# A hybrid decoder step on one core: weight sums moved from GpSimd to VectorE, up sums kept unsplit, split down halves kept in scratch, five longer raw buffers

## The chip, the cores and the metric

The kernel runs on one core of one Trainium2 chip. The metric is the device time of one execution in microseconds (us), here the median of three runs. One more execution was recorded by the hardware profiler; all rows below are from it.

## The reference, cut to what matters

The program is one layer of a decoder for 2048 prompt tokens and 8 x 4 sample tokens, width 1024: a mixer (gated linear attention beside a spatial gating unit), cross-attention over 256 memory tokens, and a gated MLP with a causal depthwise convolution over time. The change touches the last of these:

```
def conv_ffn(hn, buf, w_gate, w_up, conv_w, conv_b, w_down):
    T = hn.shape[1]
    g = hn @ w_gate                                   # (T,1024) @ (1024,2816)
    gp = jnp.concatenate([buf.astype(g.dtype), g], axis=1)
    c = conv_b + sum(conv_w[j] * gp[:, j:j + T] for j in range(CONV_W))
    out = (jax.nn.gelu(c) * (hn @ w_up)) @ w_down     # w_up (1024,2816), w_down (2816,1024)
    return out, gp[:, -(CONV_W - 1):]
```

## The kernel before, in words

All data is fp32. A product is made of three TensorE matmuls on split operands (`mm3`, lines 92 to 95): each factor is split into a part rounded to the format that TensorE reads and the rest (`split`, lines 84 to 86: ScalarE makes the high half, VectorE subtracts it to get the low half), and high x high, high x low and low x high are added in PSUM.

The 2048 tokens go through the layer in four blocks of 512 (`s` = 0 to 3); 32 sample tokens ride with block 1 in the mixer and with block 2 in the MLP. A block passes mixer, cross-attention and MLP in turn. The MLP walks over 22 feature tiles of 128 in pairs (`j`) and in groups of four tiles (`GROUPS`): for each pair a gate step and an up step; the down products of a group come between the first gate and the first up step of the next one (`main`, `pend`).

Block 0 computes gate and up plainly (`fm_step`, eight k-tiles times a 512-token moving operand, 128x512 matmuls) from weights that it loads raw (512 KB units, `wload`, line 104) and splits (`wsplit`). Beside that it prepares the weights for blocks 1 to 3 (`wmake`, `seven_make`): these use a seven-product scheme (2x2 blocks of weights and tokens, seven products in place of eight), with three plain weight quadrants A11, A12, A22 and four sums S1 to S4. `seven_make` forms the sums of one raw unit in four operations (lines 152 to 155, on GpSimd, tiles `s13`, `s24`), splits them (`sh`, `sl`), and writes the split quadrants and the split sums into scratch in device memory (`w7d`, lines 160, 161, 166). `seven_step` in blocks 1 to 3 loads each of the seven as a ready tile of split halves (`seven_tile`, line 141), accumulates the products into four quadrants in a tile `Q` (own pool `qp`, two buffers) and hands these on. The down weights are loaded raw and split anew in every block, 22 units each (`down`, `down_last`).

A raw unit needs one of `NRAW` = 3 raw buffers (tag `wraw`); a buffer is free when its last reader is done. Split halves go into five buffers each (`whi`, `wlo`). `run` makes the units of later steps up to five units ahead. All DMAs are issued by SyncE (SP in the rows), in one order. A scheduler sets the order of the instructions on each engine when the program is built; each engine then runs its own list in order. The gate results leave PSUM on VectorE at line 1364 (`gate_put`), the up results at line 1416, the down results at line 1466; a group of PSUM accumulators has four banks (`accp`).

Of the kernel before, what the change touches and what calls it, by code (L numbers as in the profile page):

```python
# [30 lines left out]
NU, NT, NRAW, NW = 49, 6, 3, 5  # L31
# [6 lines left out]
def hymba_step_kernel(  # L38
# [16 lines left out]
    qp = ctx.enter_context(tc.tile_pool(name="qp", bufs=2))  # L55
# [41 lines left out]
    def wraw(name):  # L97
        return wp.tile([128, 1024], F32, tag="wraw", name=f"r_{name}", bufs=NRAW)

    def wload(w, k0, nk, m0, mw, name):  # L100
        raw = wraw(name)
        r3 = raw.rearrange("p (k m) -> p k m", k=nk) if nk * mw == 1024 else \
            raw[:, :nk * mw].rearrange("p (k m) -> p k m", k=nk)
        nc.sync.dma_start(r3, w[k0 * 128:(k0 + nk) * 128, m0:m0 + mw].rearrange("(k p) m -> p k m", p=128))
        return r3
# [27 lines left out]
    W7 = ("A11", "A12", "A22", "S1", "S3", "S2", "S4")  # L133
# [12 lines left out]
    def seven_make(raw, hi, lo, dst, u, name):  # L146
# [5 lines left out]
        pool.tensor_tensor(h3(s13, 0), a21, a22, ALU.add)  # L152
        pool.tensor_tensor(h3(s13, 1), a11, a21, ALU.subtract)
        pool.tensor_tensor(h3(s24, 0), h3(s13, 0), a11, ALU.subtract)
        pool.tensor_tensor(h3(s24, 1), a12, h3(s24, 0), ALU.subtract)
        ks = slice(2 * u, 2 * u + 2)
        for x, t in enumerate((hi, lo)):
            t = t.bitcast(F32).rearrange("p (k two) m -> p two k m", two=2)
            for k in range(2):
                nc.sync.dma_start(dst[:, k, x, ks], t[:, k, :, 0:128])  # L160
            nc.sync.dma_start(dst[:, 2, x, ks], t[:, 1, :, 128:256])
# [25 lines left out]
    def seven_step(src, get_xs, H, use, name, order=0):  # L187
# [3 lines left out]

        def fn(*ws):
            xs, w = get_xs(), dict(zip(seq, ws))
            q = qp.tile([128, 4 * TM // 2], F32, tag="Q", name=f"q_{name}")
# [3 lines left out]
            def prod(nm):  # L198
# [7 lines left out]
                for k in range(len(xs)):  # L206
                    mm3(o, w[nm][:, 0, k], w[nm][:, 1, k], *xs[k][nm], k == 0, k == len(xs) - 1)
# [34 lines left out]
        return Step(fn, [seven_tile(src[:, W7.index(nm)], f"{name}{nm}") for nm in seq])  # L242
# [180 lines left out]
    def run(steps):  # L423
# [5 lines left out]
        for i, st in enumerate(steps):  # L429
# [12 lines left out]
    w7d = {(nm, j): dp.tile([128, 7, 2, 4, 128], F32, tag=f"w7{nm}{j}", name=f"w7{nm}{j}")  # L442
           for nm in ("g", "u") for j in range(FT // 2)}
# [898 lines left out]
    def ffn_steps(B, fin=None):  # L1342
# [36 lines left out]
        def gate7(j):  # L1379
# [8 lines left out]
            return seven_step(w7d["g", j], lambda: B.hn, H, use, f"wg{s}{j}", int(j == 0))  # L1388
# [31 lines left out]
        def upp7(j):  # L1420
# [9 lines left out]
            return seven_step(w7d["u", j], lambda: B.hn, H, use, f"wup{s}{j}")  # L1430

        def down_last(f0, half_of):
# [17 lines left out]
            return Step(fn, [(w_down[0], f0, 2, j * 512, 512, f"wd{s}{f0}{j}") for j in range(2)])  # L1450

        def down(f0, nf, m):
# [17 lines left out]
            return Step(fn, [(w_down[0], f0, nf, m * 128, nm * 128, f"wd{s}{f0}{m}")])  # L1470
# [138 lines left out]
```

## Time and profile before

| | |
|---|---|
| median of 3 runs | 2974.5 us (2973.43 to 2977.55) |
| profiled execution, device time | 2971.9 us |
| its span (first to last instruction) | 2970.2 us |
| TensorE busy | 2880.4 us, 97% of the span |
| VectorE, ScalarE, GpSimd busy | 1815.1, 1073.9, 861.9 us |
| moved by DMA | 614 MB, 207 GB/s over the span |

How to read it: PE is TensorE, PEld its weight loads, DVE VectorE, ACT ScalarE, POOL GpSimd, SP SyncE. An engine's busy time is the union of its instructions; the end of a matmul is modelled, so PE that is busy without a break can still run below its best rate. PEclk is the clock that TensorE was granted, as a share of its full speed. A row that ends in "<-" names what ended the idle time before an instruction. The MLP of block 0 lies between 420 and 820 us of the span, the others between about 1210 and 1600, 1935 and 2290, 2615 and 2970 us.

### The profile page before, as it was taken

The page shows a single profiled execution, that of the slowest core. Times are in us where ns is not written, and L with a number is a line of the kernel's source. Part 1 is how long each engine was busy: PE and PEld are TensorE (multiplying, and loading weights), DVE is VectorE, ACT ScalarE, POOL GpSimd, SP SyncE. Part 2 cuts the span into 40 slices and gives each one's busy share as a digit, 9 for nine tenths or more (in the row PEclk, how much of TensorE's full clock was granted, in tenths as well). Part 3 has the DMA queues.
Part 4 walks back from the last instruction along what each step waited for, and adds up shares of the span by engine and source line. Part 5 has one row for each costly group of instructions (what it writes and reads, how often), then busy time and mean ns, then how long its engine had stood idle before and what let it go on. Part 6 is the DMA issues. An engine that isn't in the chain of part 4 may idle for free.

```text
span 2970.2 us, 47609 instructions
## 1 busy us (share of the span) xinstructions
PE 2880.4 (97%) x18148; PEld 2534.4 (85%) x18148; DVE 1815.1 (61%) x2973; ACT 1073.9 (36%) x1948; POOL 861.9 (29%) x900
## 2 busy tenths in 40 slices
PE   8998999999999999999999999999999999999998
PEld 8787887777778789888887888899999788999997
DVE  6577558776656553654556685575557676375556
ACT  5535335343354332422223543332223543241222
POOL 1123227555422220421221232232222233041221
PEclk9999999999999899999999999999999999999999
DMA  9555679999941135887886323577775323577883
GB/s 286 180 156 159 212 233 286 276 300 295 287 130 57 52 107 176 287 295 258 305 314 200 100 72 125 195 250 252 267 264 182 112 71 108 185 276 256 286 289 127
DMA packets 389580, 613.97 MB, mean 207 GB/s; under 512 B 27195, under 2 KB 269822, under 8 KB 389352
## 3 DMA queue, kind: packets, MB, share of 16 engines
q1 hardware_dynamic: 389352, 610.92, 62.0%
q8 instruction: 144, 2.36, 0.3%
q14 instruction: 84, 0.69, 0.1%
HBM read 497.04 MB, written 113.78 MB: 206 GB/s over the span
## 4 chain that ended last, share of the span: by engine, by line
PE 75%; DVE 9%; DMA 6%; POOL 3%; ACT 3%; issue 3%; SPq 1%; DVEq 0%; POOLq 0%; ACTq 0%
PE d L94 5%; PE d L95 5%; PE d L93 5%; PE sc L94 2%; PE sc L95 2%; PE sc L93 2%; PE a_wo L94 2%; PE a_wo L95 2%; PE a_wo L93 2%; PE s L921 1%; PE a_wx L94 1%; PE a_wx L93 1%; PE a_wx L95 1%; PE a_wu L94 1%; PE a_wu L93 1%
## 5 line engine op out<-in xcount | busy, mean ns | idle before, releaser
L93 PE MATMUL d<-acth,h_wd 128*128 128x512 f32 (+2 forms) x896 | 316.1, 356 | 20.2 <-DVE g L1364 8.8
L94 PE MATMUL d<-actl,h_wd 128*128 128x512 f32 (+2 forms) x896 | 316.1, 353 | 4.7 <-DVE actl L86 4.7
L95 PE MATMUL d<-acth,l_wd 128*128 128x512 f32 (+2 forms) x896 | 315.1, 353 | 0.0
L1466 DVE TENSOR_TENSOR h<-d,h 128x512 f32<-128x512 f32 (+1 forms) x232 | 133.2, 583 | 187.4 <-PE d L95 186.6
L93 PEld LDWEIGHTS d<-acth,h_wd 128*128 128x128 f32 x896 | 170.1, 191 | 48.3 <-DVE g L1364 10.7
L94 PEld LDWEIGHTS d<-actl,h_wd 128*128 128x128 f32 x896 | 171.2, 191 | 28.3 <-DVE actl L86 6.0
L95 PEld LDWEIGHTS d<-acth,l_wd 128*128 128x128 f32 x896 | 171.1, 191 | 24.8 <-issue 2.5
L1427 POOL TENSOR_TENSOR c<-q_wup,c 128x512 f32<-128x512 f32 (+1 forms) x33 | 58.3, 1766 | 424.7 <-DVE q_wup L238 245.6
L1405 POOL TENSOR_TENSOR c<-c,bc_f 128x512 f32<-128x512 f32 (+1 forms) x88 | 129.1, 1469 | 96.3 <-ACT c L1404 87.7
L86 DVE TENSOR_TENSOR l_wd<-r_wd,h_wd 128x1024 fp32r<-128x1024 f32 x88 | 123.1, 1399 | 41.0 <-ACT h_wd L85 29.6
L95 PE MATMUL sc<-whi_qk,wol 128*128 128x256 f32 x512 | 144.1, 282 | 0.0
L93 PE MATMUL sc<-whi_qk,woh 128*128 128x256 f32 x512 | 144.0, 283 | 0.0
L94 PE MATMUL sc<-wlo_qk,woh 128*128 128x256 f32 x512 | 143.7, 282 | 0.0
L85 ACT ACTIVATE h_wd<-r_wd 128x1024 fp32r<-128x1024 f32 x88 | 92.8, 1056 | 124.4 <-PE d L94 45.1
L914 POOL TENSOR_TENSOR e<-e,k 128x512 f32<-128x512 f32 (+1 forms) x48 | 72.6, 1513 | 216.8 <-DVE kr L910 129.4
L1395 ACT ACTIVATE c<-g,colsb 128x512 f32<-128x512 f32 x88 | 71.5, 814 | 156.5 <-DVE g L1364 94.7
L93 PE MATMUL a_wo<-ch,h_wo 128*128 128x512 f32 (+1 forms) x320 | 113.4, 361 | 8.5 <-ACT ch L85 5.9
L94 PE MATMUL a_wo<-cl,h_wo 128*128 128x512 f32 (+1 forms) x320 | 114.4, 358 | 0.1
L95 PE MATMUL a_wo<-ch,l_wo 128*128 128x512 f32 (+1 forms) x320 | 113.7, 356 | 0.0
L1396 DVE SCALAR_TENSOR_TENSOR c<-g,colsb,c 128x512 f32<-128x512 f32 x88 | 90.8, 1032 | 28.7 <-ACT c L1395 27.6
L1392 POOL COPY carry<-g 128x2 f32<-128x2 f32 x88 | 34.7, 394 | 241.4 <-DVE g L1364 237.9
L93 PE MATMUL a_wx<-pTh,whi_wx 128*128 128x512 f32 x256 | 101.3, 396 | 0.0
(3282 smaller groups left out, 9455.8 us busy)
## 6 DMA issues: line engine op xcount, KB each, us to landing
r_wd<-in_w_down_dram SPq DMA_DIRECT2D x88, 512.0 KB
r_wo<-in_w_out_dram SPq DMA_DIRECT2D x32, 512.0 KB
whi_qk<-qkd SPq DMA_DIRECT2D x32, 512.0 KB
wlo_qk<-qkd SPq DMA_DIRECT2D x32, 512.0 KB
wlo_wx<-vod SPq DMA_DIRECT2D x32, 512.0 KB
whi_wx<-vod SPq DMA_DIRECT2D x32, 512.0 KB
r_wg<-in_w_gate_dram SPq DMA_DIRECT2D x22, 512.0 KB
r_wup<-in_w_up_dram SPq DMA_DIRECT2D x22, 512.0 KB
```

The lines of the kernel that those rows point to most:

```text
L85: act.activation(hi, src, AF.Copy)
L86: (lo_eng or dve).tensor_tensor(lo, src, hi.bitcast(F32), ALU.subtract)
L93: pe.matmul(ps, wh, xh, start=first, stop=False)
L94: pe.matmul(ps, wh, xl, start=False, stop=False)
L95: pe.matmul(ps, wl, xh, start=False, stop=last)
L914: pool.tensor_tensor(kl[:, :Tl], e[:, :Tl], B.k[p][:, :Tl], ALU.mult)
L1392: pool.tensor_copy(carry[:, f, :], g[:, SB:SB + 2])
L1395: act.activation(c[:, :SB], g[:, 2:SB + 2], AF.Identity, bias=cb, scale=w2)
L1396: dve.scalar_tensor_tensor(c[:, :SB], g[:, 1:SB + 1], w1, c[:, :SB], ALU.mult, ALU.add)
L1405: pool.tensor_tensor(c[:, :T], c[:, :T], B.fbc[:, :T], ALU.mult)
L1427: (dve, pool)[i].tensor_tensor(c[:, :T], q[i], c[:, :T], ALU.mult)
L1466: dve.tensor_tensor(B.h[m + mm][:, cs], ps[:, :cw], B.h[m + mm][:, cs], ALU.add)
```

## The change

The four sum operations run on VectorE. The sums of the up weights are written to scratch as they are (half the bytes of their split form) and split in each of blocks 1 to 3 when they are loaded again (`seven_sums`: one raw unit of 512 KB holds two sums); those of the gate weights stay split. The down weights are split in block 0 alone; their halves are written to scratch (`wkeep`, 2 x 512 KB per unit) and loaded ready in blocks 1 to 3 (`wready`). The quadrant tile `Q` comes out of the raw pool, which has five buffers of 1088 elements in place of three of 1024 and two `Q` buffers. The core of the diff:

```diff
-NU, NT, NRAW, NW = 49, 6, 3, 5
+NU, NT, NRAW, NW = 49, 6, 5, 5
...
-    qp = ctx.enter_context(tc.tile_pool(name="qp", bufs=2))
...
-        return wp.tile([128, 1024], F32, tag="wraw", name=f"r_{name}", bufs=NRAW)
+        return wp.tile([128, 2 * TM], F32, tag="wraw", name=f"r_{name}", bufs=NRAW)
...
+    def wkeep(dst, *spec):
+        def load():
+            out = wunit(*spec)
+            for x, t in enumerate(out):
+                nc.sync.dma_start(dst[:, x], t.bitcast(F32))
+            return out
+        return load
...
-        pool.tensor_tensor(h3(s13, 0), a21, a22, ALU.add)
-        pool.tensor_tensor(h3(s13, 1), a11, a21, ALU.subtract)
-        pool.tensor_tensor(h3(s24, 0), h3(s13, 0), a11, ALU.subtract)
-        pool.tensor_tensor(h3(s24, 1), a12, h3(s24, 0), ALU.subtract)
+        dve.tensor_tensor(h3(s13, 0), a21, a22, ALU.add)
+        dve.tensor_tensor(h3(s13, 1), a11, a21, ALU.subtract)
+        dve.tensor_tensor(h3(s24, 0), h3(s13, 0), a11, ALU.subtract)
+        dve.tensor_tensor(h3(s24, 1), a12, h3(s24, 0), ALU.subtract)
...
         for i, t in enumerate((s13, s24)):
+            d = sums[:, 2 * i:2 * i + 2]
+            put = lambda d, t: nc.sync.dma_start(d[:, :, ks], t.rearrange("p (s k m) -> p s k m", s=2, k=2))
+            if len(sums.shape) == 4:
+                put(d, t[:, :512])
+                continue
             sh, sl = U(f"sh{i}{name}", F32R), U(f"sl{i}{name}", F32R)
             split(sh[:, :512], sl[:, :512], t[:, :512])
             for x, o in enumerate((sh, sl)):
-                nc.sync.dma_start(dst[:, 3 + 2 * i:5 + 2 * i, x, ks],
-                                  o[:, :512].bitcast(F32).rearrange("p (s k m) -> p s k m", s=2, k=2))
+                put(d[:, :, x], o[:, :512].bitcast(F32))
...
+    def seven_sums(src, name):
+        def load():
+            raw = wraw(name)
+            nc.sync.dma_start(raw[:, :1024], src.rearrange("p s k m -> p (s k m)"))
+            return wsplit(raw[:, :1024].rearrange("p (k m) -> p k m", k=8), name)
+        return load
...
-            q = qp.tile([128, 4 * TM // 2], F32, tag="Q", name=f"q_{name}")
+            q = wraw(f"q_{name}")
...
-            return Step(fn, [(w_down[0], f0, nf, m * 128, nm * 128, f"wd{s}{f0}{m}")])
+            name = f"wd{s}{f0}{m}"
+            return Step(fn, [wready(wdd[f0, m], name) if s else
+                             wkeep(wdd[f0, m], w_down[0], f0, nf, m * 128, nm * 128, name)])
```

The change moves instructions on four engines; three places show how. In block 0, at the start of the down products of one group, GpSimd had the sums of two up units between its other work (`r_wup` raw unit, `c` and `g` tiles of the convolution, `carry` its two last tokens):

```order
L1405 TENSOR_TENSOR c_6239<-c_6239,bc_f_4615 128x512
L152 TENSOR_TENSOR s13wup_6329<-r_wup_6323 128x256
L153 TENSOR_TENSOR s13wup_6329<-r_wup_6323 128x256
L154 TENSOR_TENSOR s24wup_6330<-s13wup_6329,r_wup_6323 128x256
L1392 COPY carry<-g_6378 128x2
L1353 COPY g_6413<-carry 128x2
L155 TENSOR_TENSOR s24wup_6330<-r_wup_6323,s24wup_6330 128x256
L152 TENSOR_TENSOR s13wup_6429<-r_wup_6423 128x256
```

At the same place VectorE's list now holds them, between the gate evictions (line 1364 before, 1408 now), the convolution (1440, 1441) and the low halves of the down weights (`l_wd`):

```order
L1408 TENSOR_TENSOR g_6313<-a_wg_6288,bc_f_4636 128x512
L160 TENSOR_TENSOR s13wup_6274<-r_wup_6268 128x256
L161 TENSOR_TENSOR s13wup_6274<-r_wup_6268 128x256
L162 TENSOR_TENSOR s24wup_6275<-s13wup_6274,r_wup_6268 128x256
L1440 SCALAR_TENSOR_TENSOR c_6317<-g_6313,colsb,c_6317 128x512
L163 TENSOR_TENSOR s24wup_6275<-r_wup_6268,s24wup_6275 128x256
L1441 SCALAR_TENSOR_TENSOR c_6317<-g_6313,colsb,c_6317 128x512
L160 TENSOR_TENSOR s13wup_6364<-r_wup_6358 128x256
L161 TENSOR_TENSOR s13wup_6364<-r_wup_6358 128x256
L85 TENSOR_TENSOR l_wd_6263<-r_wd_6260,h_wd_6262 128x1024
L162 TENSOR_TENSOR s24wup_6365<-s13wup_6364,r_wup_6358 128x256
L1408 TENSOR_TENSOR g_6348<-a_wg_6323,bc_f_4636 128x512
```

Between the two gate evictions there now stand seven sum operations, two convolution steps and one split; a raw unit that lands late holds up what follows on VectorE, and no longer on GpSimd. SyncE's list at the same group, before (raw loads at line 104, writes of the ready tiles `w7g`):

```order
L160 DMA w7g_190<-h_wg_6141 128x2x128 x2
L161 DMA w7g_190<-h_wg_6141 128x2x128
L160 DMA w7g_190<-l_wg_6142 128x2x128 x2
L161 DMA w7g_190<-l_wg_6142 128x2x128
L104 DMA r_wd_6251<-in_w_down_dram 128x4x256
L104 DMA r_wd_6317<-in_w_down_dram 128x4x256
L104 DMA r_wup_6323<-in_w_up_dram 128x4x256
L104 DMA r_wup_6423<-in_w_up_dram 128x4x256
L166 DMA w7u_201<-sh0wup_6341 128x2x256
```

And now (raw loads at line 102, `wd_0`, `wd_2`, ... the kept down halves, line 134):

```order
L134 DMA wd_0_233<-h_wd_6108 128x1024
L102 DMA r_wup_6268<-in_w_up_dram 128x4x256
L134 DMA wd_0_233<-l_wd_6109 128x1024
L102 DMA r_wup_6358<-in_w_up_dram 128x4x256
L134 DMA wd_2_234<-h_wd_6186 128x1024
L134 DMA wd_2_234<-l_wd_6187 128x1024
L102 DMA r_wg_6406<-in_w_gate_dram 128x4x256
L134 DMA wd_4_235<-h_wd_6194 128x1024
L134 DMA wd_4_235<-l_wd_6195 128x1024
L102 DMA r_wg_6464<-in_w_gate_dram 128x4x256
L172 DMA s7u_208<-s13wup_6274 128x2x256
```

Both up units and both following gate units are now issued ahead of the writes of the first up unit's sums; before, the two gate units came behind these. In blocks 1 to 3 the four raw down loads of a group (for one group of block 2 they stood in a row) become eight loads into split buffers, with the raw sums of the next up steps (line 203) among them:

```order
L203 DMA r_wup24S_19853<-s7u_200 128x1024
L148 DMA wg24S_19721<-s7g_198 128x1024
L148 DMA wg24A_19719<-w7g_197 128x1024
L148 DMA wg24A_19723<-w7g_197 128x1024
L124 DMA whi_wd_19725<-wd_0_229 128x1024
L124 DMA wlo_wd_19727<-wd_0_229 128x1024
L124 DMA whi_wd_19729<-wd_2_230 128x1024
L124 DMA wlo_wd_19731<-wd_2_230 128x1024
L203 DMA r_wup24S_19993<-s7u_200 128x1024
L203 DMA r_wup25S_20243<-s7u_204 128x1024
```

The first raw sums of an up step stand ahead of the down halves of the group before, the second ones behind two of the four units. TensorE's instructions are the same in number and nearly the same in order.

## Rows read from the trace of the kernel before

**Rows 1.** The page's busy time of each engine, whole span.

```profile
PE 2880.4 (97%) x18148; PEld 2534.4 (85%) x18148; DVE 1815.1 (61%) x2973; ACT 1073.9 (36%) x1948; POOL 861.9 (29%) x900
```

**Rows 2.** Windows: stretch, length, busy us of each engine, PEclk, DMA share, GB/s.

```profile
420.00:820.00 400.00, 381.58 (x1621) 305.30 (x1620) 288.43 (x318) 172.00 (x241) 234.22 (x243) 0.98 0.93 287
...
1935.00:2290.00 355.00, 352.57 (x2804) 351.70 (x2803) 223.47 (x412) 91.95 (x145) 92.47 (x137) 1.00 0.72 250
```

**Rows 3.** Waits of PE, 420 to 820 us: us in total, times, longest.

```profile
PE d L93 <- DVE g L1364: 8.8, 4, 3.5
PE d L93 <- DVE h L1466: 4.0, 4, 1.6
PE d L93 <- ACT acth L85: 2.9, 1, 2.9
```

**Rows 4.** Timeline of PE behind one such wait: start us, us, instruction.

```profile
728.46 0.50 PE L93 MATMUL d<-acth,h_wd 128*128 128x512 f32 x1 [3.48 <-DVE g L1364]
...
733.14 0.40 PE L94 MATMUL d<-actl,h_wd 128*128 128x512 f32 x1
...
735.91 0.40 PE L94 MATMUL d<-actl,h_wd 128*128 128x512 f32 x1
```

**Rows 5.** Chain of waits, 700 to 760 us: start us, us, what.

```profile
705.97 4.57 DMA w7g<-h_wg
710.55 1.24 DVE l_wd L86
711.80 4.58 DMA r_wup<-in_w_up_dram
716.51 0.73 POOL s13wup L152
...
718.72 1.22 POOL s24wup L155
...
727.81 0.61 DVE g L1364
```

**Rows 6.** Groups of POOL by shape, 420 to 820 us: the largest and smallest of sums.

```profile
L155 POOL TENSOR_TENSOR s24wup<-r_wup,s24wup 128x256 f32<-128x256 f32 x22 | 26.2, 1191 | 1.3
...
L152 POOL TENSOR_TENSOR s13wg<-r_wg 128x256 f32<-128x256 f32 x20 | 18.0, 899 | 39.6 <-DMA r_wg<-in_w_gate_dram 32.6 <-DVE l_wup L86 3.9 <-issue 3.1
```

**Rows 7.** Line 174 (first group of a VectorE line: ns min/median/max, starts, forms).

```profile
L174 DVE TENSOR_TENSOR t<-wxg x12: 406/414/434, 1195.9 to 2612.3; 128x256 f32<-128x256 f32 x8, 128x272 f32<-128x272 f32 x4
```

**Rows 8.** Groups by shape, 420 to 820 us: splits of the up sums.

```profile
L86 DVE TENSOR_TENSOR sl0wup<-s13wup,sh0wup 128x512 fp32r<-128x512 f32 x22 | 21.4, 974 | 21.7 <-ACT sh0wup L85 21.4
L86 DVE TENSOR_TENSOR sl1wup<-s24wup,sh1wup 128x512 fp32r<-128x512 f32 x22 | 20.9, 949 | 11.5 <-ACT sh1wup L85 11.3
...
L85 ACT ACTIVATE sh0wup<-s13wup 128x512 fp32r<-128x512 f32 x22 | 13.9, 630 | 42.2 <-POOL s13wup L153 38.2 <-DMA w7u<-l_wup 3.9
```

**Rows 9.** Waits of POOL for raw units, 420 to 820 us.

```profile
POOL s13wup L152 <- DMA r_wup<-in_w_up_dram: 39.4, 6, 10.9
...
POOL s13wg L152 <- DMA r_wg<-in_w_gate_dram: 32.6, 7, 9.7
```

**Rows 10.** DMA issues: count, KB each.

```profile
r_wd<-in_w_down_dram SPq DMA_DIRECT2D x88, 512.0 KB
...
w7u<-sh0wup SPq DMA_DIRECT2D x22, 256.0 KB
```

**Rows 11.** Windows of 20 us: slowest and fastest with full DMA share; block 1's fastest.

```profile
660.00:680.00 20.00, 19.90 (x84) 15.80 (x83) 14.43 (x17) 8.01 (x11) 11.26 (x12) 0.97 1.00 302
740.00:760.00 20.00, 19.82 (x86) 15.82 (x86) 11.46 (x14) 6.73 (x10) 11.32 (x14) 1.00 1.09 343
...
1460.00:1480.00 20.00, 20.00 (x172) 20.00 (x171) 10.45 (x17) 3.91 (x7) 5.18 (x7) 1.00 1.03 410
```

**Rows 12.** The page's costliest groups: splits of the down weights, all blocks.

```profile
L86 DVE TENSOR_TENSOR l_wd<-r_wd,h_wd 128x1024 fp32r<-128x1024 f32 x88 | 123.1, 1399 | 41.0 <-ACT h_wd L85 29.6 <-PE a_wup23S L95 1.1 <-DMA wg26A<-w7g 1.1
...
L85 ACT ACTIVATE h_wd<-r_wd 128x1024 fp32r<-128x1024 f32 x88 | 92.8, 1056 | 124.4 <-PE d L94 45.1 <-DMA r_wd<-in_w_down_dram 24.7 <-PE a_wg L95 4.8
```

More of the change, by code (lines that the diff above doesn't have):

```diff
@@ L124, in load @@
             for x, tag in enumerate(("whi", "wlo")):
-                t = wp.tile([128, 4, 256], F32R, tag=tag, name=f"{tag}_{name}")
+                t = wp.tile(list(src.shape[0:1]) + list(src.shape[2:]), F32R, tag=tag, name=f"{tag}_{name}")
                 nc.sync.dma_start(t.bitcast(F32), src[:, x])
@@ L144, in seven_tile, with seven_make @@
         return load
-    def seven_make(raw, hi, lo, dst, u, name):
+    def seven_make(raw, hi, lo, plain, sums, u, name):
         v = raw.rearrange("p (k two) m -> p two k m", two=2)
@@ L185, in seven_tokens, with seven_step, half @@
         return out
-    def seven_step(src, get_xs, H, use, name, order=0):
+    def seven_sums(src, name):
[4 more added lines that the diff above has]
+        return load
+    def seven_step(plain, sums, get_xs, H, use, name, order=0):
         seq = (("A11", "S2", "S1", "S3", "A12", "S4", "A22"), ("A11", "S1", "A12", "S2", "S3", "S4", "A22"))[order]
         joint = 2 * H <= 512
-        def fn(*ws):
-            xs, w = get_xs(), dict(zip(seq, ws))
-            q = qp.tile([128, 4 * TM // 2], F32, tag="Q", name=f"q_{name}")
+        units, at = [], {}
+        for nm in seq:
+            if nm in PLAIN or len(sums.shape) == 5:
+                at[nm] = len(units), None
+                units.append(seven_tile(plain[:, PLAIN.index(nm)] if nm in PLAIN else sums[:, SUMS.index(nm)],
+                                        f"{name}{nm}"))
+            elif nm not in at:
+                i = SUMS.index(nm) // 2
+                for j in range(2):
+                    at[SUMS[2 * i + j]] = len(units), j
+                units.append(seven_sums(sums[:, 2 * i:2 * i + 2], f"{name}{nm}"))
+        def fn(*ws):
+            def half(nm, x, k):
+                u, j = at[nm]
+                return ws[u][:, x, k] if j is None else ws[u][x][:, 4 * j + k]
+            xs = get_xs()
+            q = wraw(f"q_{name}")
             q0, q1, q2, q3 = (q[:, i * H:(i + 1) * H] for i in range(4))
@@ L206, in prod @@
                 for k in range(len(xs)):
-                    mm3(o, w[nm][:, 0, k], w[nm][:, 1, k], *xs[k][nm], k == 0, k == len(xs) - 1)
+                    mm3(o, half(nm, 0, k), half(nm, 1, k), *xs[k][nm], k == 0, k == len(xs) - 1)
             def got(nm):
@@ L241, in fn @@
             use(q[:, 0:2 * H], q[:, 2 * H:4 * H])
-        return Step(fn, [seven_tile(src[:, W7.index(nm)], f"{name}{nm}") for nm in seq])
+        return Step(fn, units)
     def rstd_of(out, ss, p, n, inv):
@@ L591, in load @@
             hi, lo = wsplit(raw, name)
-            seven_make(raw, hi, lo, dst, u, name)
+            seven_make(raw, hi, lo, *dst, u, name)
             return hi, lo
@@ L1449, in fn @@
                         st.fn()
-            return Step(fn, [(w_down[0], f0, 2, j * 512, 512, f"wd{s}{f0}{j}") for j in range(2)])
+            return Step(fn, [wready(wdd[f0, 4 * j], f"wd{s}{f0}{j}") for j in range(2)])
         def down(f0, nf, m):
```

25 lines of the change are left out of this document (16 added, 9 removed).

## The prediction

> **What bounds the kernel now.** I read the page first. TensorE is busy for 97% of the span [rows 1], so an edit that leaves its instructions alone, as this one does, can win only what TensorE loses: idle time, and time at a lower clock behind idle time. Next the windows by stage, to see where it loses any. In the MLP of block 2 it is idle for 355 - 352.6 = 2.4 us; in that of block 0 for 400 - 381.6 = 18.4 us [rows 2]. Block 0 is also where most of the change sits, so the rest of the reading is about 420 to 820 us.
>
> How far is that stage from its floor? Behind a wait the matmuls settle at 12 steps in 735.91 - 733.14 = 2.77 us, 0.231 us each [rows 4]. The stage has 1621 matmul records [rows 2]: 1621 x 0.231 = 374 us. It takes 400, so 26 us are lost: 18 of waiting and some 8 of slow running. The slow running is the clock: the 13 steps between 728.46 and 733.14 us took 4.68 us where 13 x 0.231 = 3.0 would do, right behind a wait of 3.48 us [rows 4]; the window's granted clock is 0.98 of full speed [rows 2].
>
> What does TensorE wait for? The waits of the stage name VectorE's evictions (gate 8.8 us, down 4.0) and the high half of an activation, 2.9 [rows 3]; nobody waits for a weight directly. The chain of waits says why VectorE is late: a write of split halves to scratch (4.57 us) frees the buffer for `l_wd`, that frees the raw buffer, the raw up unit is loaded (4.58 us), GpSimd forms the four sums (716.51 to 719.94, 3.4 us), and VectorE gets to the gate eviction of TensorE's next bank only at 727.81 [rows 5]. So the stage is bound by TensorE with a loop behind it: three raw buffers, the load, slow sums, VectorE's queue.
>
> **The change part by part, block 0.** *Sums.* GpSimd loses eight groups of 20 or 22 operations, the largest 26.2 us, the smallest 18.0 [rows 6], together 173 of its 234 us [rows 2, 6]. VectorE gains 44 raw units x 4 = 176 operations on 128x256. The nearest row, a VectorE difference of two operands in SBUF of that size, has a median of 414 ns [rows 7]: 176 x 0.414 = +73 us. The up sums are no longer split here: VectorE loses 21.4 + 20.9 = 42 us, ScalarE twice 13.9 = 28 us [rows 8]. The relief from GpSimd beside it is not a row; its bounds: nothing, or, taking the 15% by which a 512-element split (974 ns) exceeds two 256-element operations (828 ns) [rows 7, 8] as what GpSimd costs and 173/234 of it as gone, 0.15 x 288 x 0.74 = 32 us. I take the middle, 16, since no row lies nearer to one end. VectorE then has 288 + 73 - 42 - 16 = 303 us (287 to 319), below 374: busier, not the bound.
>
> *Raw buffers.* No quadrant tile lives in block 0, so five buffers serve the raw loads where three did; by SyncE's order the next units are issued a group of writes earlier. The 13 waits for raw units that GpSimd had (72 us, the longest 10.9) [rows 9] are what this is worth in lateness; on TensorE's path they are part of the 26 us, not added to it. Had they stayed, they would now stand in VectorE's list, ahead of evictions; that is a rival below.
>
> *Transfers.* The stage moves 287 GB/s x 400 us = 114.8 MB [rows 2]. Kept down halves add 22 units x 2 x 512 KB = 23.1 MB; the unsplit up sums save half of four groups of 22 x 256 KB, 11.5 MB [rows 10]. New: 126.3 MB. Seven of the twenty 20-us windows of this stage ran at a DMA share of 1.00 or more; they moved 302 to 343 GB/s [rows 11], 321 in the mean of the seven. At the mean 126.3 MB take 393 us, at the ends 418 and 368. The new writes are in whole rows of 4 KB; block 1, whose loads are mostly in such rows, reached 410 GB/s in a window [rows 11], and with 23.1 MB at that rate and 103.2 at 321 the stage needs 56 + 322 = 378 us. I take 384, between 378 and 393. So the transfers, not TensorE's 374, become what the stage lasts for, and of the 26 us lost 400 - 384 = 16 come back. Writes that trail behind the last products cost nothing: the stage behind has transfers to spare.
>
> The Trainium skill's page "DMA: Bandwidth & Descriptors", section "Specifications", gives about 358 GB/s as the HBM limit of one core; by that 126.3 MB would take an estimated 353 us, below TensorE's floor, and all 26 us would come back. The trace does not bear the figure out as a limit, since a window of block 1 stands at 410 [rows 11], and it does not say that smaller pieces get there, since block 0's best is 343. The outcome it points to is the first rival.
>
> **Blocks 1 to 3.** Each drops 22 splits of down units and gains 11 up steps x 2 = 22 splits of raw sums of the same 128x1024 shape: 66 x 1056 ns on ScalarE and 66 x 1399 ns on VectorE [rows 12] go and come back, zero in sum. In bytes: 66 x 512 KB more for down halves, 33 up steps x 2 x 512 KB less for sums, zero as well. What hides the moved splits is that SyncE issues the raw sums ahead of the down halves of the group before. Without that cover each of the 33 up steps could wait one split pair, 1.06 + 1.40 = 2.5 us [rows 12]: 0 to +81 us. I take 0, the value nearest to the 2.4 us that TensorE idles in all of block 2's MLP with as many splits [rows 2]. Down loads now wait at SyncE for a free split buffer, with raw sums queued behind them; two down units ahead of the second raw sum is the longest such queue, and it is let go as TensorE finishes. The quadrant tile in the raw pool takes two of five buffers in a pair of steps and the raw sums two: zero, with the same price if it is short. Mixer and attention: zero, within 5 us either way, since the scheduler has set the lists anew.
>
> **The sum.** 2971.9 us of the profiled execution (span 2970.2 and 1.7 around it) - 16 = 2956. The median of the runs shown is 2.6 above the profiled one, so 2974.5 - 16 = 2958.5; I predict 2958.
>
> **Rivals.**
> *All of it comes back.* The transfers keep ahead of TensorE, as at 343 GB/s (368 us) [rows 11], and the stage falls to 374: 2974.5 - 26 = 2948. For it: 410 in block 1, whole rows. Against: 103 of the 126 MB keep their small pieces.
> *Transfers pace block 0, and it gets slower.* With 126.3 MB the stage lasts longer than 400 us if the sustained rate is below 126.3/400 = 316 GB/s. At 302, the slowest full window [rows 11], it takes 418: 2974.5 + 18 = 2992. For it: the stage's mean is 287 today, with a DMA share of 0.93 already [rows 2]. Against: the share is below 1 because three raw buffers hold the issue back, and in windows without that the rate is above 316 in the mean.
> *The wait moves to VectorE.* Raw units land late as now, and VectorE, in whose list their sums stand, waits 72 us in 13 pieces where GpSimd did [rows 9]. Four PSUM banks of twelve matmuls cover 4 x 12 x 0.231 = 11 us in the down products, about the longest wait, so TensorE would lose about what it loses now: no change, 2974. For it: VectorE's load rises. Against: five buffers.
> *Blocks 1 to 3 lose.* If a third of the 33 up steps wait 2.5 us, +27 eats the gain: 2974.5 + 11 = 2985. Against: block 2 hides the same splits today.
>
> **How the numbers follow.** Forecast 0.48, all back 0.17, slower by transfers 0.15, moved to VectorE 0.14, lost in blocks 1 to 3 0.06. Within 0.2% means within 6 us, about what a measurement of this kernel can tell from no change. Faster: forecast (but 0.02 of it) and all back, 0.63. Same: 0.14 + 0.02 + 0.01 = 0.17. Slower: 0.15 + 0.05 = 0.20. The range starts at 2943 (all back, and 5 us from the other stages) and goes to 2982, which leaves out the worse half of the slower cases, about 0.15. The forecast's own range is 2974.5 - 26 to 2974.5 - 7 (the 393 us): 2948 to 2967.
>
> **What would show it.** Right: in block 0's MLP the waits of TensorE for gate and down evictions shrink, matmuls run at 0.231 us, the DMA share is near 1 with over 316 GB/s, waits for raw units are gone, and the stage is 375 to 393 us long; VectorE's sums take about 0.41 us; the MLPs of blocks 2 and 3 keep their length. Wrong: TensorE waits for splits of raw units (transfers too slow), VectorE's first sum waits for `r_wup` or `r_wg`, or TensorE idles in blocks 1 to 3 ahead of the products of S1 to S4 or of `d`.

## The result and the profile after

The changed kernel takes 2935.3 us (median of four runs, 2927.4 to 2940.1) where the kernel before takes 2976.0 beside it: a ratio of 0.986, 95% interval 0.9835 to 0.9885, or 41 us less. The forecast was 2958, in a range of 2943 to 2982. The direction was right; the gain was two and a half times the forecast one, and the time lies outside the range.

The windows view of the profile after, the MLP of block 0 (us, then busy time and instructions of PE, PEld, DVE, ACT and POOL, granted clock, DMA share, GB/s), and under it the same stage of the kernel before, both from TensorE's first gate product to its last down product:

```profile
434.00:804.00 370.00, 370.00 (x1620) 301.31 (x1619) 277.88 (x440) 147.11 (x199) 64.46 (x71) 1.00 1.02 333
```
```profile
440.00:839.00 399.00, 380.30 (x1630) 304.35 (x1629) 285.12 (x328) 171.59 (x248) 220.27 (x231) 0.98 0.91 279
```

TensorE is busy without a break at full clock, for 370 us. Its waits for gate and down evictions [rows 3] are gone: in this window the waits view of TensorE has no row left. The transfers run at a share of 1.02 and 333 GB/s, so they are close to a limit of their own, but what the stage lasts for is still TensorE. The 20-us windows that answer to [rows 11]:

```profile
660.00:680.00 20.00, 20.00 (x88) 16.27 (x87) 12.97 (x19) 7.59 (x10) 6.06 (x6) 1.00 0.98 294
...
740.00:760.00 20.00, 20.00 (x88) 16.25 (x87) 10.97 (x15) 6.78 (x9) 3.14 (x4) 1.00 1.05 331
760.00:780.00 20.00, 20.00 (x87) 16.17 (x87) 14.61 (x22) 5.71 (x7) 1.53 (x2) 1.00 1.06 387
```

TensorE loses no time in any of them, not even in the one at 294 GB/s. What VectorE waits for in this stage (engine, line, what it waited for: us in all, times, longest) answers to GpSimd's waits in [rows 9]:

```profile
DVE s13wup L160 <- DMA r_wup<-in_w_up_dram: 17.1, 9, 5.4
DVE s13wg L160 <- DMA r_wg<-in_w_gate_dram: 12.5, 5, 4.7
```

The waits for raw units did move to VectorE, 30 us in 14 pieces in place of 72 us in 13, and TensorE feels none of them.

Where the 44.6 us between the two profiled executions (spans 2970.2 and 2925.6) went, by the times at which TensorE starts and ends a stage in the two traces:

| stretch | before | after | difference |
|---|---|---|---|
| start of the span to block 0's MLP | 439.7 | 433.7 | -6.0 |
| block 0's MLP | 399.0 | 370.2 | -28.8 |
| its end to block 1's MLP | 373.0 | 366.4 | -6.6 |
| block 1's MLP | 414.8 | 410.4 | -4.4 |
| the rest, blocks 2 and 3 | 1343.7 | 1344.8 | +1.1 |

So 29 us came where the forecast put 16, and 17 us, of which blocks 2 and 3 take 1 back, where it put zero. TensorE's instructions are as many as before [rows 1]:

```profile
PE 2861.2 (98%) x18148; PEld 2530.0 (86%) x18148; DVE 1819.1 (62%) x3105; ACT 1049.9 (36%) x1904; POOL 698.1 (24%) x724
```

Of the 44.6 us, 25.4 are idle time of TensorE, and 19.2 are the same instructions in less busy time. In block 0's MLP the two are 18.7 and 10, outside it 7 and 9.

### The profile page after: what moved, and what is told of

It reads as the page before. It is cut to its first block, busy times and chain, and to the rows that moved or that the text cites. A ratio compares the mean times of both kernels' runs of the same rounds, so it can differ in the third digit from the quotient of the medians.

```text
span 2925.6 us, 47483 instructions
## 1 busy us (share of the span) xinstructions
PE 2861.2 (98%) x18148; PEld 2530.0 (86%) x18148; DVE 1819.1 (62%) x3105; ACT 1049.9 (36%) x1904; POOL 698.1 (24%) x724
## 4 chain that ended last, share of the span: by engine, by line
PE 90%; DVE 5%; DMA 1%; issue 1%; ACT 1%; POOL 1%; SPq 0%; DVEq 0%; POOLq 0%; ACTq 0%
PE d L94 6%; PE d L93 6%; PE d L92 6%; PE a_wo L92 2%; PE a_wo L94 2%; PE a_wo L93 2%; PE sc L94 2%; PE sc L93 2%; PE sc L92 2%; PE a_wx L92 2%; PE a_wx L93 2%; PE a_wx L94 2%; PE a_wg L94 1%; PE a_wg L93 1%; PE a_wup L94 1%; PE a_wg L92 1%
## 5 line engine op out<-in xcount | busy, mean ns | idle before, releaser
L92 PE MATMUL d<-acth,whi_wd 128*128 128x512 f32 (+2 forms) x720 | 242.2, 340 | 4.8 <-ACT acth L84 4.8
L93 PE MATMUL d<-actl,whi_wd 128*128 128x512 f32 (+2 forms) x720 | 242.6, 338 | 1.4 <-DVE actl L85 1.4
L94 PE MATMUL d<-acth,wlo_wd 128*128 128x512 f32 (+2 forms) x720 | 242.1, 337 | 0.0
L1449 POOL TENSOR_TENSOR c<-c,bc_f 128x512 f32<-128x512 f32 (+1 forms) x88 | 137.0, 1558 | 149.9 <-ACT c L1448 149.9
L1471 POOL TENSOR_TENSOR c<-r_q_wup,c 128x512 f32<-128x512 f32 (+1 forms) x33 | 60.1, 1821 | 410.9 <-DVE r_q_wup L274 264.6
L92 PEld LDWEIGHTS d<-acth,whi_wd 128*128 128x128 f32 x720 | 134.9, 188 | 20.2 <-ACT acth L84 5.3
L94 PEld LDWEIGHTS d<-acth,wlo_wd 128*128 128x128 f32 x720 | 135.6, 188 | 16.2 <-issue 2.1
L93 PEld LDWEIGHTS d<-actl,whi_wd 128*128 128x128 f32 x720 | 135.6, 188 | 15.9 <-DVE actl L85 1.9
L1436 POOL COPY carry<-g 128x2 f32<-128x2 f32 x88 | 29.9, 340 | 418.6 <-DVE g L1408 416.5
L93 PE MATMUL a_wx<-pTl,whi_wx 128*128 128x512 f32 x256 | 100.4, 392 | 0.0
L94 PE MATMUL a_wx<-pTh,wlo_wx 128*128 128x512 f32 x256 | 100.4, 392 | 0.0
```

The costliest lines, as they stand in the source:

```text
L92: pe.matmul(ps, wh, xh, start=first, stop=False)
L93: pe.matmul(ps, wh, xl, start=False, stop=False)
L94: pe.matmul(ps, wl, xh, start=False, stop=last)
L1436: pool.tensor_copy(carry[:, f, :], g[:, SB:SB + 2])
L1449: pool.tensor_tensor(c[:, :T], c[:, :T], B.fbc[:, :T], ALU.mult)
L1471: (dve, pool)[i].tensor_tensor(c[:, :T], q[i], c[:, :T], ALU.mult)
```

## The experiments

The change has four parts: (A) five longer raw buffers, with `Q` in their pool; (B) the sums on VectorE; (C) up sums unsplit in scratch; (D) down halves kept. All runs, with the stage times read from each trace as in the table above. A ratio is to the kernel before on the same chip, whose median was between 2966 and 2976 us there; kernels are compared by ratio. The stage times of a row are from one execution, and executions of one kernel differ by up to 21 us (the kernel before, 2960.8 to 2981.7 us on one chip). The profiled one is the fastest of its kernel in six rows, after and after_again among them, and the slowest in o2_dve_sums and u3_up_split. Block 0's MLP repeats within 0.1 us (after, after_again, v_vr); the stretch from its end to block 1's MLP differs by 2.4 us between two executions of the same kernel, so small differences there are not told from scatter.

| kernel | parts | ratio to before (95%) | block 0's MLP starts at | lasts | to block 1's MLP | block 1's MLP |
|---|---|---|---|---|---|---|
| before | none | 1 | 439.7 | 399.0 | 373.0 | 414.8 |
| o1_five_raw | A | 0.9955 (0.9942 to 0.9967) | 431.1 | 386.6 | 370.0 | 414.0 |
| o2_dve_sums | B | 0.9939 (0.9925 to 0.9952) | 440.3 | 383.2 | 371.2 | 415.9 |
| o3_up_unsplit | C | 1.0008 (0.9995 to 1.0021) | 438.1 | 387.0 | 371.1 | 422.7 |
| x_two | A, B | 0.9905 (0.9893 to 0.9918) | 432.4 | 375.7 | 364.8 | 414.8 |
| u1_three_raw | B, C, D | 0.9959 (0.9943 to 0.9976) | 444.5 | 376.6 | 367.5 | 417.3 |
| u2_pool_sums | A, C, D | 0.9900 (0.9881 to 0.9919) | 433.7 | 371.5 | 375.4 | 413.1 |
| u3_up_split | A, B, D | 0.9959 (0.9947 to 0.9972) | 432.8 | 395.9 | 381.3 | 416.5 |
| u4_down_raw | A, B, C | 0.9878 (0.9857 to 0.9899) | 432.1 | 371.2 | 372.5 | 414.2 |
| after | all | 0.9860 (0.9835 to 0.9885) | 433.7 | 370.2 | 366.4 | 410.4 |
| after_again | all | 0.9879 (0.9860 to 0.9898) | 431.9 | 370.2 | 364.0 | 410.2 |
| e_keep_twice | all, D twice | 1.0075 (1.0063 to 1.0087) | 431.8 | 411.1 | 386.8 | 412.6 |
| v_sums_raw | all, gate sums unsplit too | 0.9949 (0.9935 to 0.9964) | 433.7 | 371.5 | 372.9 | 419.9 |
| v_vr | all | 0.9893 (0.9876 to 0.9909) | 431.6 | 370.2 | 372.6 | 411.8 |
| v_vr_downraw | A, B, C | 0.9907 (0.9892 to 0.9921) | 432.9 | 371.4 | 368.0 | 414.5 |
| v_vr2 | all | 0.9879 (0.9861 to 0.9896) | 425.1 | 368.9 | 370.7 | 413.2 |
| v_vr2_downraw | A, B, C | 0.9884 (0.9858 to 0.9909) | 426.4 | 370.3 | 366.5 | 414.1 |

### One part taken back

**u1_three_raw**, three raw buffers, of 1024 elements again:

```diff
-NU, NT, NRAW, NW = 49, 6, 5, 5
+NU, NT, NRAW, NW = 49, 6, 3, 5
+    qp = ctx.enter_context(tc.tile_pool(name="qp", bufs=2))
-            q = wraw(f"q_{name}")
+            q = qp.tile([128, 4 * TM // 2], F32, tag="Q", name=f"q_{name}")
```

> The changed kernel with one part undone: three raw buffers of 1024 elements and an own pool of two buffers for the quadrant tile. Theory A (the five raw buffers are the main part: in block 0 they break the loop of raw load, sums, splits and evictions, and outside it they give the gains that the prediction set at zero, 6 us ahead of block 0's MLP and 11 us in block 1): nearly all is lost again, about 2965 us, with TensorE waiting for gate and down evictions in block 0's MLP (stage back from 370 to over 390 us). Theory B (the sums on GpSimd were what made VectorE late): block 0's MLP stays at 370 to 375 us and only the 17 us outside are lost: about 2950 us.

It loses 1.0% of the 1.4%, but only 6 us of that in block 0's MLP (376.6, near the second theory's 370 to 375): the most is lost ahead of it, which starts 11 us later, and some 7 in block 1's. The total is near the first theory's 2965, so neither holds as a whole. Waits of TensorE from 60 us to block 0's MLP, in u1_three_raw:

```profile
PE qkp L93 <- ACT wqh L85: 4.0, 1, 4.0
PE mvt L552 <- DVE mvf L543: 2.9, 2, 2.5
PE a_wo L93 <- DVE r L783: 2.7, 1, 2.7
PE sctp L434 <- DVE mko L553: 2.4, 1, 2.4
```

The first three stand in the kernel before too; in after the first is left with 1.3 us and the second with 0.5. Idle time is 6 of the 11 us (28.7 for 22.3 up to the stage's start); the other 4 to 5 are slower running. Raw buffers serve every stage that loads raw weights, the memory products and the mixer of block 0 too.

**u2_pool_sums**, the sums back on GpSimd (four lines `dve.tensor_tensor` to `pool.tensor_tensor`):

```diff
-        dve.tensor_tensor(h3(s13, 0), a21, a22, ALU.add)
+        pool.tensor_tensor(h3(s13, 0), a21, a22, ALU.add)
```

> The changed kernel with the four sum operations back on GpSimd. Theory A (raw buffers): within 6 us of the changed kernel, 2935 to 2942, block 0's MLP 370 to 376 us. Theory B (sums on GpSimd make VectorE late): block 0's MLP goes back to 390 us or more, about 2958 us. Either way VectorE's two-operand operations in that stage get longer again beside GpSimd: the 1024-element splits from a mean near 1.22 us to about 1.4.

Block 0's MLP keeps its 371 us: with the other three parts in, it does not need the sums on VectorE. The loss of 0.4% in the ratio, about 12 us, has intervals that touch those of the whole change; in the trace most of it stands on the way to block 1's MLP (375.4 for 366.4), where its code does not differ; 4 us of that are the output projection treated below, the rest was not traced. Beside GpSimd's sums the 1024-element splits of gate and up weights got longer, from means of 1243 and 1271 ns to 1336 and 1407; those of the down weights stayed at 1310.

**u3_up_split**, up sums split before they are kept:

```diff
-[128, 4, 2, 4, 128] if nm == "g" else [128, 4, 4, 128]
+[128, 4, 2, 4, 128]
```

> The changed kernel with the up sums split in block 0 and kept split, as before. This adds 11.5 MB of writes and 44 splits on ScalarE and VectorE to block 0's MLP, and takes 66 splits away from blocks 1 to 3. If transfers pace block 0's MLP (it moved 333 GB/s at a DMA share of 1.02 for 370 us), 11.5 MB more take 35 us, of which writes that trail behind hide some: plus 15 to 30 us, 2950 to 2965. If transfers are hidden and TensorE alone is the bound: within 6 us, 2930 to 2941.

**u4_down_raw**, down weights raw in every block:

```diff
-wready(wdd[f0, m], name) if s else wkeep(wdd[f0, m], w_down[0], f0, nf, m * 128, nm * 128, name)
+(w_down[0], f0, nf, m * 128, nm * 128, name)
```

> The changed kernel with the down weights loaded raw and split in every block, nothing kept. This takes 23 MB of writes out of block 0's MLP. TensorE is busy without a break there already, so in block 0 both theories say no change (stage 370 us, transfers down to about 290 GB/s). If the kept halves are what shortened block 1's MLP by 4 us, plus 4 us: 2939; if that came from the buffers, 2935.

The two belong together. u3_up_split moves 11.5 MB more in block 0 and loses 26 us there; u4_down_raw moves 23.1 MB less and wins nothing there. Windows of block 0's MLP, u3_up_split and u4_down_raw:

```profile
433.00:829.00 396.00, 379.81 (x1632) 305.63 (x1630) 304.42 (x491) 172.83 (x245) 56.33 (x71) 0.98 1.03 333
```
```profile
432.00:803.00 371.00, 370.99 (x1628) 301.86 (x1627) 276.98 (x442) 148.81 (x204) 70.37 (x71) 1.00 0.88 270
```

At a share of 0.88 TensorE sets the 371 us; at 1.03 something else sets 396. But u3_up_split also has more splits on VectorE, which is busy for 304 us in place of 278, so the bytes were not shown by it alone.

### Bytes or splits

**x_two**, A and B alone (u3's and u4's edits together): all the splits of u3_up_split, 23.1 MB less.

```diff
-[128, 4, 2, 4, 128] if nm == "g" else [128, 4, 4, 128]
+[128, 4, 2, 4, 128]
-wready(wdd[f0, m], name) if s else wkeep(wdd[f0, m], w_down[0], f0, nf, m * 128, nm * 128, name)
+(w_down[0], f0, nf, m * 128, nm * 128, name)
```

> The kernel after with two of its four parts only: five longer raw buffers and the sums on VectorE. The up sums are split before they are kept, and the down weights are loaded raw and split in every block, both as in the kernel before. Block 0's MLP then has the bytes of the kernel before (115 MB by its rows) and all of the splits that u3_up_split had. Theory 'transfers' (u3_up_split lost 26 us in block 0's MLP because it moved 11.5 MB more): here the stage is back at 370 to 373 us, whole kernel 2935 to 2942. Theory 'splits' (u3_up_split lost it because VectorE and ScalarE split the up sums in the chain of the weights): the stage stays at 390 to 396 us, whole kernel 2958 to 2965.

**e_keep_twice**, the whole change with each down half written twice:

```diff
-wdd[f0, m] = dp.tile([128, 2, nf, 1024 // nf]
+wdd[f0, m] = dp.tile([128, 4, nf, 1024 // nf]
-            for x, t in enumerate(out):
+            for x, t in enumerate(out * 2):
```

> The kernel after, with each kept down half written to scratch twice, to two places, of which the second is never read: 23 MB more of writes in block 0's MLP, nothing added on any compute engine. Theory 'transfers pace the stage as soon as it moves more than 333 GB/s x 370 us = 123 MB': 149 MB at 333 to 348 GB/s take 429 to 448 us, so the stage grows by 59 to 78 us and the kernel is at 2994 to 3013. Theory 'only what the compute engines do on the way to the weights counts': no change, 2932 to 2942.

Windows of block 0's MLP, x_two and then e_keep_twice:

```profile
432.00:808.00 376.00, 373.89 (x1630) 303.23 (x1629) 306.95 (x487) 175.38 (x249) 68.41 (x71) 1.00 0.95 297
```
```profile
432.00:843.00 411.00, 380.12 (x1632) 307.34 (x1630) 276.28 (x446) 144.38 (x200) 62.83 (x71) 0.96 1.03 341
```

VectorE's load is the same in x_two (307 us) and u3_up_split (304), the stage is 376 against 396: it was the 23.1 MB of kept halves, and not the splits (the first theory, though the stage is 3 us longer than its 370 to 373, and the gain by the ratio, 28 us, is 5 short of its 33). Whether the bytes themselves count or the split buffers that their stores hold was not separated by this pair. e_keep_twice adds nothing to a compute engine and loses 41 us in the stage; TensorE waits there for splits of weights that land late (first fence), and the trailing writes hold up a load at the start of block 1 (second, 830 to 870 us):

```profile
PE a_wg L92 <- ACT h_wg L84: 12.3, 2, 6.8
PE d L92 <- ACT h_wd L84: 11.9, 1, 11.9
PE a_wup L92 <- ACT h_wup L84: 6.5, 1, 6.5
```
```profile
PE xts L722 <- DMA x<-in_x_sample_dram: 12.4, 1, 12.4
```

Its span is 63.7 us longer than after's; 23.1 MB at the 341 GB/s of the row are 68. The stage itself grew by 41 where 59 to 78 were expected; the rest fell on block 1's start, to which the writes trail. That the whole growth fits the added bytes speaks for the bytes. This is what a stage paced by transfers looks like, and the kernel after is just short of it: 11.5 MB more (u3_up_split) already cost 26 us.

### One part alone on the kernel before

**o1_five_raw** and **o2_dve_sums** take over, of the diff in the section on the change, only these lines (o1 with `Q` in the raw pool):

```diff
-NU, NT, NRAW, NW = 49, 6, 3, 5
+NU, NT, NRAW, NW = 49, 6, 5, 5
```
```diff
-        pool.tensor_tensor(h3(s13, 0), a21, a22, ALU.add)
+        dve.tensor_tensor(h3(s13, 0), a21, a22, ALU.add)
```

> The kernel before with one part of the change: five longer raw buffers. Sums on GpSimd, up sums split and kept split, down weights raw in every block, as before. Theory A (the raw buffers carry most, and taking them away from the whole change cost 25 us): 2948 to 2955, most of it ahead of and in block 0's MLP. Theory B (the parts only work together: sums on GpSimd beside VectorE's splits keep the weights late): 2966 to 2975.

> The kernel before with one part of the change: the weight sums on VectorE. Three raw buffers, up sums split, down weights raw. Theory A (each part has its own price, sums about 9 us): 2964 to 2969. Theory B (the prediction's rival: with three raw buffers the raw units land late and VectorE now waits for them ahead of evictions, and it gets 73 us of sums on top of 288): no gain or a loss, 2974 to 2990.

**o3_up_unsplit** has C alone:

```diff
-[128, 4, 2, 4, 128]
+[128, 4, 2, 4, 128] if nm == "g" else [128, 4, 4, 128]
```

> The kernel before with one part of the change: the up sums are kept unsplit and split at use. Three raw buffers, sums on GpSimd, down weights raw. Block 0's MLP moves 103 MB in place of 115 and VectorE and ScalarE lose 42 and 28 us of splits there; blocks 1 to 3 split 66 raw sums more. Theory A (fewer bytes and fewer splits shorten the loop from write to raw load): block 0's MLP at 380 to 390 us, blocks 1 to 3 unchanged, whole kernel 8 to 18 us faster than before. Theory B (the loop is bound by raw buffers and GpSimd's sums alone, and blocks 1 to 3 pay for the splits): within 5 us of before or slower.

Each of A, B and C alone takes 12 to 16 us off block 0's MLP, and any two of them 22 to 28 (x_two, u1_three_raw and u2_pool_sums; u3_up_split is over the bytes): they shorten the same loop [rows 5] at different links, and any two nearly close it. Only A moves the start of that stage (431.1; the kernels with five buffers start it at 431 to 434, v_vr2's pair earlier, those with three at 438 to 445). In the whole, o1_five_raw brings 13 us, between its two theories (20 to 27, and 0 to 9), o2_dve_sums 18, more than either of its theories, and x_two 28: the two are nearly additive. The rival by which VectorE would lose what GpSimd lost, with three raw buffers, fell. C alone comes out at nothing, since block 1's MLP loses 8 us and block 2's and 3's 3 each. Waits of its block-1 MLP (1196 to 1619 us):

```profile
PE d L93 <- ACT acth L85: 5.0, 1, 5.0
PE d L93 <- ACT h_wd L85: 2.8, 1, 2.8
PE a_wup11A L93 <- DMA wup11A<-w7u: 2.1, 1, 2.1
```

With five buffers (u4_down_raw) the same splits leave block 1's MLP at 414.2, and the second and third wait are missing; the first is there too, with 5.1 us. So it is the raw buffers that hide most of it; the splits themselves are no cheaper.

**v_sums_raw**, the gate sums unsplit as well:

```diff
-[128, 4, 2, 4, 128] if nm == "g" else [128, 4, 4, 128]
+[128, 4, 4, 128]
```

> The kernel after, with the gate sums kept unsplit and split at use as well: 11.5 MB less in block 0's MLP, 42 us less of splits on VectorE there and 28 on ScalarE, and 66 splits more of 128x1024 in blocks 1 to 3 on each. Theory A (the splits at use are hidden beside the products, as those of the up sums were): the same as after within 5 us, since block 0's MLP already stands at TensorE's 370 us. Theory B (VectorE and ScalarE have no room left in blocks 1 to 3, where a MLP has splits of gate, up or down in every step): slower than after by 10 us or more.

The second theory: block 0's MLP keeps its 371 us with 11.5 MB less, and the MLPs of blocks 1 to 3 lose 9.5, 4.2 and 6.9 us, for 66 pairs of splits more. So further splits at use are not free in those blocks.

### The wait that came in

In the stretch ahead of block 0's MLP (60 to 434 us), the kernel after has a wait of 7.9 us that takes 0.4 in the kernel before:

```profile
PE vop L92 <- DMA vr<-vd: 7.9, 1, 7.9
```

It comes with the five raw buffers: 6.4 to 7.9 us in every kernel that has them (but v_vr2 and v_vr2_downraw), at most 1.6 in those with three. SyncE issues this load of value rows behind sixteen stores in a row, the last of which are:

```profile
279.87 0.60 SPq L612 DMA_DIRECT2D vod<-vol  x1
280.53 0.42 SPq L612 DMA_DIRECT2D vod<-voh  x1
281.00 0.44 SPq L612 DMA_DIRECT2D vod<-vol  x1
281.54 0.89 SPq L561 DMA_DIRECT2D vr<-vd  x2
```

**v_vr** issues it one half head earlier, **v_vr2** at the start of the head before:

```diff
         if jh == 0:
-            again("v", h)
-        vh, vl = mem_st.t["v"]
+            if h == 0:
+                again("v", 0)
+            mem_st.t["vnow"] = mem_st.t["v"]
+            if h < 3:
+                again("v", h + 1)
+        vh, vl = mem_st.t["vnow"]
```

(v_vr has the second `again` in the branch for `jh == 1`.)

> The kernel after, with the load of the value rows of the next head in block 0's memory stage issued one half head earlier, so that TensorE need not wait for it (7.9 us at some 278 us in the profile after). Theory A (that wait is on the path and nothing else takes its place): 7 to 8 us faster than after, 2927 to 2929, ratio to before about 0.9835. Theory B (what bounds the stretch is the mixer's weights, and TensorE waits for them a little later instead): within 3 us of after, 2932 to 2938.

> v_vr with the down weights loaded raw and split in every block, as in the kernel before (u4_down_raw and v_vr together). u4_down_raw was level with after. Theory A (kept down halves are worth nothing, and the stretch ahead of block 0's MLP gains from fewer writes): level with v_vr within 3 us. Theory B (the 4 us that block 1's MLP had over u4_down_raw are real): 4 us slower than v_vr.

> The kernel after, with the load of the next head's value rows issued ahead of the 16 stores of the folded halves of this head (v_vr put it behind the first 8 of them and behind the 8 of the other half, where it stood in SyncE's list as before: its wait stayed at 7.4 us). Theory A (the 7.9 us wait is on the path): it goes, block 0's MLP starts at 425 to 427 us, and the kernel is 7 us faster than after, ratio about 0.9840 where after has 0.9863. Theory B (TensorE waits for the mixer's weights a little later instead): the wait goes, and the MLP of block 0 still starts within 2 us of after's.

> v_vr2 with the down weights loaded raw and split in every block. Whether kept down halves are worth anything: u4_down_raw stood 4 us over after in its ratio, v_vr_downraw 4 us over v_vr. If that is real, this is 4 us slower than v_vr2; if it was scatter, level within 3 us.

> The kernel after itself, once more, on the chip on which v_vr2 and v_vr2_downraw run, so that these can be compared with it there. In the first comparison its ratio to before was 0.986. If block 0's MLP gives 29 us, its front 8 and block 1 the rest, for reasons of the program, the profile shows the same stages again within 1 us each (block 0's MLP 370, its start at 433 to 434, block 1's mixer to MLP 358). If the 8 us of block 1 come from chance in a run, they are gone or elsewhere.

v_vr missed its aim: its load was issued behind the same stores, and the wait stayed at 7.4 us. v_vr2 has it at 1.4:

```profile
PE t_wr L92 <- ACT u L787: 2.0, 1, 2.0
PE vop L92 <- DMA vr<-vd: 1.4, 1, 1.4
```

Block 0's MLP then starts 7 us earlier than in after_again and ends 8 earlier, but at block 1's MLP only 1.4 us of it are left and at the end none: 0.9879 against 0.9879. Part of what is given back can be read in block 1's output projection. TensorE's waits there, v_vr2 (996 to 1074 us) and after_again (1001 to 1076 us):

```profile
PE a_wo L92 <- ACT ch L84: 3.1, 1, 3.1
PE ops L1064 <- DMA sg<-in_state_gla_dram: 0.9, 1, 0.9
```
```profile
PE ops L1060 <- DMA sg<-in_state_gla_dram: 1.1, 1, 1.1
```

The wait for `ch` (1.9 us in the kernel before, 3.2 in u4_down_raw) is missing in after and after_again alone. Both executions of that kernel lack it, so it is no chance of one run. ScalarE makes `ch` from `z`, a product that GpSimd forms. The last `z` ahead of that wait, in v_vr2 and in after (start us, us, instruction):

```profile
1013.49 6.36 POOL L861 TENSOR_TENSOR z<-z,u 128x544 f32<-128x544 f32 x1 [2.46 <-DVE z L857]
```
```profile
1023.58 1.39 POOL L857 TENSOR_TENSOR z<-z,u 128x544 f32<-128x544 f32 x1 [2.46 <-DVE z L853]
```

In both kernels it starts 0.15 us behind the first of twenty VectorE operations with two operands in SBUF (`o<-o,ors,r`), and the lists of VectorE, ScalarE and GpSimd stand in the same order there. In v_vr2, in u1_three_raw and in every other kernel with five raw buffers it ends only after all twenty; in after and after_again it runs at once, and the second VectorE operation takes 1.42 us in its place. (In before, o2_dve_sums and o3_up_unsplit it is started behind the twenty.) What lets GpSimd in first in the one program was not found.

The kept down halves are worth nothing that these runs can tell. In all three pairs the kernel with them is ahead, by 5 us (after, u4_down_raw), 4 (v_vr, v_vr_downraw) and 1.5 (v_vr2, v_vr2_downraw: 0.9879 against 0.9884), each within the intervals. No kernel tried beats the one with the whole change.

## Why the prediction failed

**What bounds the kernel: right.** TensorE with a loop behind it, in block 0's MLP; 18.7 us of waiting and 10 of slow running came back there, where 18 and 8 were counted. The floor was put 4 us too high: 1620 records now take 370 us, 0.228 each, for the 0.231 taken from 2.77 us of a row [rows 4], since 36 of them are smaller than 128x512. The window of 420 to 820 us was laid 20 us ahead of the stage, which is at 439.7 to 838.7 in the kernel before (block 2's MLP is at 1926.3 to 2305.5, and TensorE idles 3.9 us in it, not 2.4).

**Transfers in block 0: the first step that failed.** "I take 384": transfers do have a floor, and e_keep_twice and u3_up_split stand on it, but it was put too high. So "the transfers, not TensorE's 374, become what the stage lasts for" did not come true: TensorE is busy for all of the 370 us, and u4_down_raw, with 23.1 MB less, takes 371.2. Two sizes were off.

The bytes: the stage's own window of before moved 279 GB/s x 399 us = 111 MB, not the 114.8 of the window ahead of it. With 11.5 more that is 123, and the row after shows 333 x 370 = 123. At 333 GB/s the 126.3 MB of the forecast would take 379 us, so these 3 MB are 9 of the 14 us. The rate: 126.3 MB in 384 us are 329 GB/s, and the stages on the floor sustain 333 (u3_up_split) and 341 (e_keep_twice). The seven windows of before [rows 11] averaged 321 at a mean share of 1.04; with the kept halves, written in rows of 4 KB, about the same share moves more (341 at 1.03 in e_keep_twice; without them u4_down_raw moves 270 at 0.88, an estimated 307 at a full share). Of the prices in the text the one by the highest row, 343 GB/s and 368 us, came nearest. The rival "all of it comes back" is what happened in this stage; it put 26 us on it, and 29 came.

The Trainium skill's page "DMA: Bandwidth & Descriptors", section "Specifications", with its 358 GB/s for one core, pointed to that rival. The runs agree with its outcome and not with the figure as a limit, for a 20-us window of after moved 387 GB/s.

**Sums on VectorE: right in price, low in relief.** The eight groups of sums average 418 to 473 ns for the 414 forecast. VectorE's busy time is 278 us, below the forecast's 287 to 319. Group by group (the mean before less the mean after, times the count in the stage) the relief from GpSimd is 28 us, where I took 16 and held 32 for the bound. The rest is counting: 160 of the 176 sums stand in the stage, and busy time is a union in which the short sums overlap their neighbours (the durations add up to 304 us in after, 303 before). The split of gate sums, in before, after and u2_pool_sums (ns min/median/max):

```profile
L86 DVE TENSOR_TENSOR sl0wg<-s13wg,sh0wg x20: 675/898/1228, 449.0 to 767.9; 128x512 fp32r<-128x512 f32 x20
```
```profile
L85 DVE TENSOR_TENSOR sl0wg<-s13wg,sh0wg x20: 676/683/693, 436.8 to 729.4; 128x512 fp32r<-128x512 f32 x20
```
```profile
L85 DVE TENSOR_TENSOR sl0wg<-s13wg,sh0wg x20: 675/693/1799, 436.3 to 736.6; 128x512 fp32r<-128x512 f32 x20
```

Alone it takes 683 ns; beside GpSimd's weight sums it reaches 1228 in the kernel before. The 1799 of u2_pool_sums is beside GpSimd's product of the convolution (`c`), not a sum; after has such a case too, 1780 ns in the other split of the gate sums, beside a third product of GpSimd (`wxsq`). The gate eviction, which reads one operand from PSUM, does not change: 22 of them average 681 ns before, 686 after. The Trainium skill's page "SBUF — State Buffer", section "SBUF: two separate sides", says so: a VectorE instruction with two inputs in SBUF and a GpSimd instruction that reads SBUF exclude each other for a whole instruction. The traces agree: the splits of 1.2 us and over that start during a GpSimd operation end 0.55 us behind its end (in the kernel before, one of 1.22 us starts at 449.00, during a sum that ends at 449.66), and the 6.36 us of `z` above are the same exclusion the other way round.

**Raw buffers: right in block 0's MLP, wrong in scope.** They were counted for that stage alone. Ahead of it five buffers bring 7 to 9 us (o1_five_raw, x_two), although the wait for value rows comes in with them; without that wait, in v_vr2, the stage starts 15 us earlier than before. "Mixer and attention: zero, within 5 us either way" is the second step that failed, and the one that put the time outside the range: with 29 us for block 0's MLP and zero elsewhere it would have been 2974.5 - 29 = 2945.5. The 6.0 us ahead of that stage, 6.6 behind it and 4.4 in block 1's MLP did the rest.

**Blocks 1 to 3: zero was right for the whole, by cover and not for nothing.** The splits did cost: 8 us in block 1 alone with three raw buffers, 21 us over three blocks with one group more. Of the 11 us gained from block 0's MLP to the end of block 1's, 4 stand in block 1's output projection (58.7 us before, 54.3 after), with the wait for `ch`, and 4 in its MLP. There the idle time hardly differs (6.2 us before, 5.3 after) and the granted clock does: 0.99 of full speed before, 1.00 in after and after_again, 0.99 in v_vr2, which idles 5.2 us. No kernel with a part left out has both, and why the clock stays up in the one program is open.

**The signs named ahead.** "VectorE's first sum waits for `r_wup` or `r_wg`" was to be a sign of failure; it came, 30 us of it, and meant nothing, as VectorE idles 92 of the 370 us. Of the signs of being right, the waits for evictions went, the sums take 0.42 to 0.47 us, the transfers reached 333 GB/s, and the MLPs of blocks 2 and 3 kept their length within 1 us; the waits for raw units did not go, and 370 us is below the 375 to 393.

## What to carry to other kernels

Where several edits shorten one loop, cost them together from the floor of the engine behind it, not one by one: here any two of three nearly closed it. A stage is priced from its own window, with its own bytes. A transfer rate read while the loop held the transfers back, and with another mix of pieces, need not be the limit, and a run that adds bytes and nothing else shows how far the limit is. A pool is shared by all stages that draw on it, so a larger one is costed over the whole program, and an engine's durations are taken with and without its neighbour beside it.

## What the runs showed of the hardware

Mixed pieces sustain 333 to 341 GB/s here for 400 us when transfers set the pace (u3_up_split, e_keep_twice), with a 20-us window of after at 387. A VectorE split of 128x512 with two operands in SBUF takes 683 ns alone, up to 1228 beside GpSimd's sums in the kernel before, and 1799 beside its convolution product in u2_pool_sums; the mean of the gate evictions from PSUM moves by 5 ns. The other way round, a GpSimd product of 128x544 takes 1.39 us in after and 6.36 in v_vr2, where twenty such VectorE operations run first.
